# MLP of layer 1 in Strassen products: VectorE's work on the next operand placed behind the running product's first tile, and up product 6 combined through psum

## The chip, the cores and the metric

The kernel runs on one core of one Trainium2 chip. The metric is the device time of one execution in microseconds. The time of the kernel before is the median of three runs.

The engines are called as the profile calls them: PE (TensorE), DVE (VectorE), ACT (ScalarE), POOL (GpSimd) and SP (SyncE, which issues most DMAs). An instruction of an engine waits in that engine's own queue: the engines work beside each other, and each takes its instructions in the program's order.

## What is computed

The program is one inference step of a decoder trunk with two layers. Each layer has a mixer (gated linear attention, then differential attention) and an MLP with a squared ReLU, each followed by a normalized residual. The changed part is the MLP of layer 1, the last long piece of the program:

```python
def post_norm(x, f, g, b):
    return layer_norm(DEEPNORM_ALPHA * x + f, g, b)

def sq_relu_mlp(x, w1, w2):
    h = jax.nn.relu(x @ w1)
    return (h * h) @ w2
...
        x_p = post_norm(x_p, sq_relu_mlp(x_p, mlp_w1[layer], mlp_w2[layer]), ln_mlp_g[layer], ln_mlp_b[layer])
```

`x_p` has 1040 rows of 1024 values (16 meta tokens and 1024 prompt tokens), `w1` is 1024 x 4096 and `w2` 4096 x 1024, all fp32. Eight further rows, the running sequences, go along.

## The kernel before

**Groups and products.** `mlp1` cuts the 4096 hidden values into four groups g of 1024. For each group it computes the hidden values ("up", with w1) and then their part of the output ("down", with w2). Either is a product of two matrices cut into 2 x 2 blocks, and is done with seven block products instead of eight, as Strassen's method does, so some operands are sums or differences of blocks (the tables `UP_W`, `UP_X`, `DOWN_H`, `DOWN_W`; "run" stands for the running sum or difference in `RW` or `RX`). The order is the list `seq`: in each group up products 1, 2, 5, 6, 4, 3, 7, then down products 1, 5, 6, 3, 7, 4, 2 (in the last group 1, 5, 6, 7, 4, 3, 2). That makes 56 products.

**Precision.** Each fp32 operand is split into a rounded part (hi) and a rest (lo), and each product is three matmuls: hi x hi (line L206), hi x lo (L207) and lo x hi (L208), in `mm3`. For the weights (`weight_operand`) ACT writes hi (`whi`, L1634) and POOL subtracts to get lo (`wlo`, L1635); terms of a sum are added by a DMA that POOL issues (L1633), and loads are issued by SP (L1631). For the activations (`chip_operand`) DVE forms the difference of blocks in `RX` (L1609), ACT casts hi (L202), and DVE subtracts hi to get lo (L203); hi and lo go to the tiles `XH`. Both kinds have two buffers, so an operand is written while the product before it runs. `chip_operand` does this in two halves, the inner blocks k = 0 and 1, then k = 2 and 3.

**Tiles.** An up product has four row blocks x two column halves, eight psum tiles of 128 x 258 with 12 matmuls each. `up_tile` then combines a tile with the sums in `HF`: ACT copies for products 1 and 5 (L1682, L1686), DVE adds and subtracts otherwise (L1679, L1680). A down product has four psum tiles of 128 x 512, 12 matmuls each, which `down_tile` adds into `Y`, for products 6 and 7 by way of `RP` (L1710, L1714). The tiles `mmt` and `axt` take turns, three buffers each.

**The running sequences.** Some products carry a "side product" (L1655): four small matmuls that read the fp32 weight tiles, which come free for new loads only after it.

**What sets the order.** The program is recorded in the order of the Python code, with the next product's operands asked for at t = 2 of the running one, and a scheduler then places each engine's instructions by its own estimate of when they are ready. `tc.issue_after(ins)` ties the instructions of its block that run on the engine of `ins` behind `ins`; it adds no wait between engines. So where DVE's steps stand decides, in the scheduler's eyes, when operands are ready, and with that the order of PE's matmuls.

Of the kernel before, what the change touches and what calls it, by code (L numbers as in the profile page):

```python
# [16 lines left out]
ALU = mybir.AluOpType  # L17
# [91 lines left out]
UP_X = {1: [(0, 0)], 2: [(1, 0)], 5: [(0, 1), (0, 0)], 6: [(1, 1), "run"], 4: [(1, 0), "run"], 3: [(1, 1)], 7: [(0, 1), (1, 1)]}  # L109
DOWN_H = {1: [(0, 0)], 2: [(0, 1)], 5: [(1, 0), (1, 1)], 6: [(0, 0), "run"], 3: [(0, 1), "run"], 4: [(1, 1)], 7: [(1, 0), (0, 0)]}  # L110
# [4 lines left out]
def hybrid_step(ctx, tc, A, dbg=None, upto=9):  # L115
    nc = tc.nc
    V, S, G, TE = nc.vector, nc.scalar, nc.gpsimd, nc.tensor
# [24 lines left out]
    def mmt():  # L142
        return banks["mm"].tile([P, 512], F32, name="mmt") if "mm" in banks else pairt()[:, 0]

    def axt():
        return banks["ax"].tile([P, 512], F32, name="axt")

    def smt():
        return banks["sm"].tile([P, 512], F32, name="smt")
# [18 lines left out]
    TH = 512 + NS // 2  # L168
# [29 lines left out]
    def kunit(w, c0):  # L198
        return unit(256, w.rearrange("(k p) n -> p k n", p=P)[:, :, c0 : c0 + 256])

    def split(hi, lo, src, eng=V):
        S.copy(hi, src)  # L202
        return eng.tensor_tensor(lo, src, hi.bitcast(F32), op=ALU.subtract)  # L203
# [139 lines left out]
    ps = smt()  # L343
# [16 lines left out]
    ps = smt()  # L360
# [202 lines left out]
    ps = smt()  # L563
# [4 lines left out]
    ps = smt()  # L568
# [8 lines left out]
    ps = smt()  # L577
# [15 lines left out]
    ps = smt()  # L593
# [5 lines left out]
    for hh in range(2):  # L599
        ps = smt()  # L600
# [13 lines left out]
    ps = smt()  # L614
# [4 lines left out]
    for s in (8, 4, 2, 1):  # L619
        u = t2()[:, :128]  # L620
        level(sb.rearrange("p h t -> p (h t)"), sqk[:, :128], sqk[:, 128:], u, s, V)
        ps = smt()
# [74 lines left out]
    ps = smt()  # L697
# [144 lines left out]
    for h in range(GH):  # L842
        hi, lo = kunit(wi, 2048 + h * 256)
        hv, lv = (w.rearrange("p (k n) -> p k n", n=256) for w in (hi, lo))
        silt = st2.rearrange("p k (c n) -> p k c n", c=2)
        for c in range(2):
            cs = slice(512 * c, 512 * c + 512)
            sil, pts = [], []
            for m in range(2):
                ps = mmt()  # L850
# [218 lines left out]
    steps_v, steps_g = [], []  # L1069
# [171 lines left out]
    for u, t2_ in ((u, t) for u in range(12) for t in range(4)):  # L1241
# [6 lines left out]
        ps = mmt()  # L1248
        for i in range(2):
            t = 2 * t2_ + i  # L1250
# [7 lines left out]
        if u < 8:  # L1258
            tmp = qt.tile([P, 2, 4, 16], F32, name="qr")
# [130 lines left out]
    ps = smt()  # L1390
# [36 lines left out]
    for step in steps + [None] * 0:  # L1427
        if step:
            h, n, t = step
            if h < 7:  # L1430
                if n == 0:
                    nxt = prep(h + 1, *raws[h + 1])
# [14 lines left out]
        at = t % 4 if h == 7 else t // 2  # L1447
        back(t, sc_, po[:, at * P : (at + 1) * P], *vals[h])
        if n % 4 == 3:
            ts = (slice(0, 4), slice(4, 8))[n // 4] if h == 7 else slice(t % 2, 8, 2)  # L1450
            S.copy(Yd[:, ts, h], po.rearrange("p (t e) -> p t e", e=P))
            for i in range(4):
                x = po[:, i * P : (i + 1) * P]
# [30 lines left out]
    HF = hp.tile([P, NB, 2, TH], F32, name="HF")  # L1484

    RX = hp.tile([P, 4 * TH], F32, name="RX")
# [9 lines left out]
    def xr(c):  # L1496
        if c == len(XR):
            XR.append(cp.tile([P, NB, TH], F32, name="XR%d" % c, tag="XL%d" % c))
        return XR[c]
# [40 lines left out]
    XF = [xr(c).rearrange("p k n -> p (k n)") for c in range(2)]  # L1540
# [51 lines left out]
    loads = []  # L1592
    sides = []

    def chip_operand(terms, quarter, n, tmp):


        parts = [x.rearrange("p k n -> p (k n)")[:, : 4 * n] for x in XH.t[count[0] % 2]]
        count[0] += 1
        hi, lo = (x.rearrange("p (k n) -> p k n", n=n) for x in parts)  # L1600
        rv, tv = (x[:, : 4 * n].rearrange("p (k n) -> p k n", n=n) for x in (RX, tmp))
        for j in (0, 2):
            b = slice(j, j + 2)
            x = quarter(*terms[0])[:, b]
            if len(terms) > 1:

                y = rv[:, b] if terms[1] == "run" else quarter(*terms[1])[:, b]
                out = (tv if terms[1] != "run" else rv)[:, b]
                V.tensor_tensor(out, x, y, op=ALU.subtract)  # L1609
                x = out  # L1610
            split(hi[:, b], lo[:, b], x)
        return hi, lo

    def weight_operand(terms, quarter, side=None):
# [29 lines left out]

    w1, w2 = A["mlp_w1"][1], A["mlp_w2"][1]

    def operands(g, up, i):
        if up:
            left = weight_operand(UP_W[i], lambda h, k: (w1, 512 * k, 1024 * g + 512 * h))
            right = chip_operand(UP_X[i], lambda k, c: xr(c)[:, 4 * k : 4 * k + 4, :], TH, RX)  # L1650
            return left, right

        def beside(k, t):
            r, u = beside.quarter
            TE.matmul(acc[u][k * TS : (k + 1) * TS, :], hs[:, 4 * r + k, :], t, start=g == 0 and i in (1, 3), stop=g == 3 and r == 1)  # L1655


        beside.quarter = ({1: (0, 0), 3: (1, 1), 7: (0, 1), 2: (1, 0)} if g < 3 else {1: (0, 0), 5: (0, 1), 6: (1, 0), 7: (1, 1)}).get(i)
        left = chip_operand(DOWN_H[i], lambda c, k: HF[:, 4 * k : 4 * k + 4, c, :512], 512, XF[0][:, : 4 * TH] if g == 3 and i == 7 else RX)
        right = weight_operand(DOWN_W[i], lambda k, u: (w2, 1024 * g + 512 * k, 512 * u), beside if beside.quarter else None)  # L1660
        return left, right

    ups = []
# [8 lines left out]
    def up_tile(g, i, m, c, left, right, ps):  # L1672
        (ah, al), (bh, bl) = left, right
        ps = ps[:, :CH]
        ms, cs = slice(m * P, (m + 1) * P), slice(c * CH, (c + 1) * CH)
        for k in range(4):
            mm3(ps, ah[:, k, ms], al[:, k, ms], bh[:, k, cs], bl[:, k, cs], k == 0, k == 3)
        c11, c12, c21, c22 = (HF[:, 4 * h + m, x, cs] for h in range(2) for x in range(2))
        add = lambda out, x, y: ups.append(V.tensor_tensor(out, x, y, op=ALU.add).ins)  # L1679
        less = lambda out, x, y: V.tensor_tensor(out, x, y, op=ALU.subtract)  # L1680
        if i == 1:
            S.copy(c12, ps)  # L1682
        elif i == 2:
            add(c11, c12, ps)
        elif i == 5:
            S.copy(c22, ps)  # L1686
        elif i == 6:
            less(c21, ps, c12)
            add(c22, c22, c21)
        elif i == 4:  # L1690
            add(c21, c21, ps)
        elif i == 3:
            less(c12, ps, c22)
        else:
            add(c22, c22, ps)
            add(c21, c21, ps)
        if c:
            for h, x in {2: [(0, 0)], 3: [(0, 1)], 7: [(1, 1), (1, 0)]}.get(i, ()):
                hidden(h, x, m)
# [28 lines left out]
    def mlp1():  # L1728
        seq = []
        for g in range(4):  # L1730
            seq += [(g, 1, i) for i in (1, 2, 5, 6, 4, 3, 7)]
            seq += [(g, 0, i) for i in ((1, 5, 6, 3, 7, 4, 2) if g < 3 else (1, 5, 6, 7, 4, 3, 2))]
        nxt = operands(*seq[0])
        n = 0
        for at, (g, up, i) in enumerate(seq):
            now = nxt
            if not up and i == 1:
                if g == 0:
                    beta = alpha_row(A["ln_mix_b"][1:2], ALU.add)
                else:  # L1740
                    for _ in range(2):
                        next(beta, None)
            if at == len(seq) - 2:
                both = {i: now, seq[-1][2]: operands(*seq[-1])}
                for x, t in ((3, 0), (3, 1), (2, 0), (3, 2), (2, 1), (3, 3), (2, 2), (2, 3)):
                    n += 1
                    down_tile(g, x, t, *both[x], axt() if n % 2 else mmt())
                    yield t, int(x == 3)
                return
            for t in range(4):  # L1750
                if t == 2:
                    nxt = operands(*seq[at + 1])
                if t == 1 and sides:
                    side, own = sides.pop(0)
                    for k in reversed(range(4)):
                        side(k, own[k])
                if up:
                    for c in range(2):
                        n += 1
                        up_tile(g, i, t, c, *now, axt() if n % 2 else mmt())  # L1760
                    if g == 0 and at in (1, 2):
                        y = Yt[:, 4 * (at - 1) + t, :]
                        with tc.issue_after(ups[-1]):
                            steps_v.append(V.scalar_tensor_tensor(y, y, ALPHA, grow, ALU.mult, ALU.mult).ins)
                    continue
                n += 1
                down_tile(g, i, t, *now, axt() if n % 2 else mmt())
                if g == 3:
                    for c, u in {7: [(1, 1)], 4: [(1, 0)]}.get(i, ()):
                        yield 4 * c + t, u  # L1770
            if g == 3 and not up and i == 7:
                samples_out()
            if g == 3 and up and i == 7:
                for x, nm in ((fg, "g"), (fb, "b")):
                    dma(x, A["ln_mlp_" + nm][1:2].broadcast_to([P, D]))
                with tc.issue_after(loads[-1]):
                    for t0, t1 in ((0, 2), (4, 8)):
                        dma(A["y_prompt"][0, t0 * P : t1 * P], A["ln_mlp_b"][1:2].broadcast_to([(t1 - t0) * P, D]))
                spare.extend(XF[0][:, 4 * TH + 512 * j : 4 * TH + 512 * (j + 1)] for j in range(4))

    normalize(mlp1(), stats, lambda c: None, last)
    e.close()
    if dbg:
# [27 lines left out]
```

## Time and profile before

| | |
|---|---|
| median of 3 runs | 2797.68 us (2791.86 to 2802.81) |
| the profiled execution | 2808.13 us |
| its span, first to last instruction | 2806.4 us |
| mean granted clock of PE | 0.991 |
| up products of group 0 | from about 2120 us |
| up products of group 1, PE never waiting | 2295.3 to 2375.8 us |
| last products | to about 2793 us, then the last normalization |

The profile comes from one execution. Its page names instructions by line, engine, operation and tiles (out<-in). A row of the view of groups gives the count, the busy time, the mean ns of one, and the idle time of the engine just before them with what ended it. A row of the timeline gives start, duration, engine, line, and in brackets the idle time before it and what released it. In the rows, a matmul's duration is longer than its distance to the next one, since matmuls are pipelined.

### The profile page before, as it was taken

How to read it: one execution, taken by the hardware profiler on the slowest of the kernel's cores; microseconds unless marked ns; L12 is line 12 of the kernel's file. 1: busy time of each engine (PE TensorE's matmuls, PEld its weight loads, DVE VectorE, ACT ScalarE, POOL GpSimd, SP SyncE). 2: the span in 40 equal slices, each digit the busy share in tenths (PEclk: the TensorE clock that was granted, in tenths of full speed). 3: DMA queues.
4: the chain of work that ended last, by engine and by line, in shares of the span. 5: the costliest groups of instructions: out<-in, count | busy, mean ns of one | idle time of the engine just before them, and what ended most of it. 6: DMA issues, size and time to landing. Idle time of an engine off the chain costs nothing. (4 is left out here: it accounts for less than half of the span.)

```text
span 2806.4 us, 52253 instructions
## 1 busy us (share of the span) xinstructions
PE 2726.4 (97%) x19849; PEld 2239.9 (80%) x19849; DVE 1941.7 (69%) x3000; ACT 1114.3 (40%) x2284; POOL 1088.1 (39%) x744
## 2 busy tenths in 40 slices
PE   8989999999999999999999999899999999999998
PEld 5867767987777777777798989777898989798986
DVE  5375362678777787777568740887647888988697
ACT  4324463152221222222242112777625646355554
POOL 2132112234344343434233312200026767666775
PEclk9999999999999999999999999999999999999999
DMA  7476545725798898888658995212144455554575
GB/s 235 166 238 217 198 153 184 261 93 186 284 334 314 310 354 300 334 318 314 243 172 305 361 368 178 65 47 80 38 126 90 103 139 112 140 119 105 133 185 120
DMA packets 276392, 562.81 MB, mean 201 GB/s; under 512 B 23510, under 2 KB 144412, under 8 KB 272044
## 3 DMA queue, kind: packets, MB, share of 16 engines
q1 hardware_dynamic: 256076, 522.75, 53.3%
q0 software_dynamic: 20064, 36.71, 8.0%
q8 instruction: 156, 2.56, 0.4%
q14 instruction: 96, 0.79, 0.1%
HBM read 533.00 MB, written 29.52 MB: 200 GB/s over the span
## 5 line engine op out<-in xcount | busy, mean ns | idle before, releaser
L194 POOL TENSOR_TENSOR wlo<-raw,whi 128x512 fp32r<-128x512 f32 x252 | 360.9, 1446 | 708.7 <-ACT whi L193 586.1
L206 PE MATMUL mmt<-whi,XH 128*128 128x256 f32 (+1 forms) x1760 | 523.9, 300 | 1.1 <-DVE ast L1338 0.9
L207 PE MATMUL mmt<-wlo,XH 128*128 128x256 f32 (+1 forms) x1760 | 522.1, 298 | 0.4 <-POOL wlo L194 0.4
L206 PE MATMUL mmt<-XH,whi 128*128 128x512 f32 (+1 forms) x1216 | 437.4, 361 | 5.9 <-DVE HL L203 2.6
L208 PE MATMUL mmt<-XH,wlo 128*128 128x512 f32 (+1 forms) x1216 | 433.9, 357 | 0.2 <-POOL wlo L1635 0.2
L208 PE MATMUL mmt<-whi,XL 128*128 128x256 f32 x1536 | 432.4, 285 | 0.0
L193 ACT CAST whi<-raw 128x512 fp32r<-128x512 f32 x252 | 150.2, 619 | 567.0 <-PE mmt L208 187.7
L206 PEld LDWEIGHTS mmt<-whi,XH 128*128 128x128 f32 x1760 | 330.5, 189 | 39.7 <-issue 24.3
L943 DVE TENSOR_REDUCE sc<-pg 128x16 f32<-128x1024 f32 x256 | 308.3, 1211 | 69.8 <-POOL pg L942 67.3
L207 PEld LDWEIGHTS mmt<-wlo,XH 128*128 128x128 f32 x1760 | 332.1, 189 | 15.7 <-issue 5.5
L942 DVE TENSOR_TENSOR pg<-pg,qb 128x1024 f32<-128x1024 f32 x192 | 270.7, 1417 | 62.1 <-DMA pg<-in_cache_k 53.5
L207 PE MATMUL mmt<-XL,whi 128*128 128x512 f32 x768 | 308.3, 402 | 0.0
L208 PEld LDWEIGHTS mmt<-whi,XL 128*128 128x128 f32 x1536 | 288.4, 189 | 7.3 <-issue 6.8
L206 PEld LDWEIGHTS mmt<-XH,whi 128*128 128x128 f32 x1216 | 230.6, 190 | 50.2 <-issue 7.6
L942 POOL TENSOR_TENSOR pg<-pg,qb 128x1024 f32<-128x1024 f32 x64 | 163.4, 2555 | 258.3 <-DMA pg<-in_cache_k 175.6
L208 PEld LDWEIGHTS mmt<-XH,wlo 128*128 128x128 f32 x1216 | 231.0, 190 | 36.4 <-issue 3.3
L206 PE MATMUL mmt<-whi,HH 128*128 128x512 f32 x512 | 204.7, 401 | 4.3 <-DVE Y L1175 3.1
L208 PE MATMUL mmt<-whi,HL 128*128 128x512 f32 x512 | 203.9, 398 | 0.0
L207 PE MATMUL mmt<-wlo,HH 128*128 128x512 f32 x512 | 203.4, 397 | 0.0
L1635 POOL TENSOR_TENSOR wlo<-RW,whi 128x512 fp32r<-128x512 f32 x96 | 162.8, 1732 | 69.8 <-ACT whi L1634 69.5
L1635 POOL TENSOR_TENSOR wlo<-rw,whi 128x512 fp32r<-128x512 f32 x92 | 154.4, 1768 | 90.1 <-ACT whi L1634 89.8
L207 PEld LDWEIGHTS mmt<-XL,whi 128*128 128x128 f32 x768 | 146.2, 190 | 39.5 <-issue 8.0
(450 smaller groups left out, 5711.7 us busy)
## 6 DMA issues: line engine op xcount, KB each, us to landing
pg<-in_cache_k SPq DMA_DIRECT2D x256, 512.0 KB
pg<-in_cache_v SPq DMA_DIRECT2D x256, 512.0 KB
raw<-in_mlp_w SPq DMA_DIRECT2D x164, 256.0 KB
swt<-in_mlp_w SPq DMA_DIRECT2D x32, 1024.0 KB
rw<-in_mlp_w SPq DMA_DIRECT2D x116, 256.0 KB
RW<-in_mlp_w POOLq DMA_DIRECT2D x96, 256.0 KB, 5.6
swt<-in_gla_w_in SPq DMA_DIRECT2D x12, 1024.0 KB
swt<-in_diff_w_in SPq DMA_DIRECT2D x12, 1024.0 KB
```

Of the source, the lines that this page charges most:

```text
L193: S.copy(hi[:, c], raw)
L194: G.tensor_tensor(lo[:, c], raw, hi[:, c].bitcast(F32), op=ALU.subtract)
L206: TE.matmul(ps, ah, bh, start=first, stop=False)
L207: TE.matmul(ps, ah, bl, start=False, stop=False)
L208: return TE.matmul(ps, al, bh, start=False, stop=last)
L942: eng.tensor_tensor(pg, pg, qb, op=ALU.mult)
L943: return V.tensor_reduce(sc[:, n, :], pg.rearrange("p (h d) -> p h d", d=64), op=ALU.add, axis=AX.X).ins
L1635: G.tensor_tensor(lo[:, k, :], t, hi[:, k, :].bitcast(F32), op=ALU.subtract)
```

## The change

Two things are changed. First, in up product 6 the difference of a psum tile and a block of `HF` is written back to psum, the second add reads it from there, and a copy brings it to `HF`; before, the difference went to `HF`, and the add read two `HF` blocks. Second, each product gets a mark: the last DVE step of its first row block (none for up products 1 and 5, which have no DVE step). The DVE steps of `chip_operand` for the next product are tied behind that mark. `less` now also records its instruction, so that it can be a mark.

```diff
-    def chip_operand(terms, quarter, n, tmp):
+    def chip_operand(terms, quarter, n, tmp, mark):
...
-                V.tensor_tensor(out, x, y, op=ALU.subtract)
+                with tc.issue_after(mark) if mark else nullcontext():
+                    V.tensor_tensor(out, x, y, op=ALU.subtract)
                 x = out
-            split(hi[:, b], lo[:, b], x)
+            with tc.issue_after(mark) if mark else nullcontext():
+                split(hi[:, b], lo[:, b], x)
...
-        less = lambda out, x, y: V.tensor_tensor(out, x, y, op=ALU.subtract)
+        less = lambda out, x, y: ups.append(V.tensor_tensor(out, x, y, op=ALU.subtract).ins)
...
         elif i == 6:
-            less(c21, ps, c12)
-            add(c22, c22, c21)
+            less(ps, ps, c12)
+            add(c22, c22, ps)
+            V.tensor_copy(c21, ps)
...
             for t in range(4):
+                if t == 1:
+                    mark = ups[-1] if up and i not in (1, 5) else None if up else steps_v[-1]
                 if t == 2:
-                    nxt = operands(*seq[at + 1])
+                    nxt = operands(*seq[at + 1], mark)
```

The order of the instructions moves on DVE and, with it, on PE. **DVE, up product 6 of group 1.** Before, from the last step of product 2 on; `RX` is the difference for the next products, `XH` the operand tiles, and `HF<-axt,HF` the first psum read of a tile of product 6:

```order
L203 TENSOR_TENSOR XH_24052<-RX,XH_86 128x1032
L1609 TENSOR_TENSOR RX<-XR_24892,RX 128x1032
L203 TENSOR_TENSOR XH_24052<-RX,XH_86 128x1032
L1609 TENSOR_TENSOR RX<-XR_24892,RX 128x1032
L203 TENSOR_TENSOR XH_23783<-RX,XH_84 128x1032
L1680 TENSOR_TENSOR HF<-axt,HF 128x258
L1609 TENSOR_TENSOR RX<-XR_25159 128x1032
L1679 TENSOR_TENSOR HF<-HF 128x258
L1680 TENSOR_TENSOR HF<-mmt,HF 128x258
L203 TENSOR_TENSOR XH_23783<-RX,XH_84 128x1032
```

Now, from the first psum read of product 6 on:

```order
L1682 TENSOR_TENSOR axt<-axt,HF 128x258
L1681 TENSOR_TENSOR HF<-HF,axt 128x258
L1692 COPY HF<-axt 128x258
L1682 TENSOR_TENSOR mmt<-mmt,HF 128x258
L1681 TENSOR_TENSOR HF<-HF,mmt 128x258
L1692 COPY HF<-mmt 128x258
L1610 TENSOR_TENSOR RX<-XR_24892,RX 128x1032 x2
L1682 TENSOR_TENSOR axt<-axt,HF 128x258
L1682 TENSOR_TENSOR mmt<-mmt,HF 128x258
L203 TENSOR_TENSOR XH_23783<-RX,XH_84 128x1032
```

Before, both differences for product 4 and the first split stood ahead of the first psum read of product 6; now they stand behind two whole tiles, and the second split of product 4 stands behind five more steps.

**DVE, from down product 5 to down product 6 of group 0.** Before; `RP` is the running sum of product 6, `XH_23783` the lo part of product 3's operand:

```order
L1609 TENSOR_TENSOR RX<-HF,RX 128x1024
L1710 TENSOR_TENSOR Y<-Y,mmt 128x512 x2
L1710 TENSOR_TENSOR Y<-Y,axt 128x512 x2
L203 TENSOR_TENSOR XH_23783<-RX,XH_84 128x1024
L1710 TENSOR_TENSOR Y<-Y,mmt 128x512 x2
L203 TENSOR_TENSOR XH_23783<-RX,XH_84 128x1024
L1609 TENSOR_TENSOR RX<-HF 128x1024 x2
L1710 TENSOR_TENSOR RP<-axt,RP 128x512
L1710 TENSOR_TENSOR RP<-mmt,RP 128x512
```

Now, from the first psum read of product 6 on:

```order
L1713 TENSOR_TENSOR RP<-axt,RP 128x512
L1713 TENSOR_TENSOR Y<-Y,RP 128x512
L1610 TENSOR_TENSOR RX<-HF,RX 128x1024
L1713 TENSOR_TENSOR RP<-mmt,RP 128x512
L1610 TENSOR_TENSOR RX<-HF,RX 128x1024
L1713 TENSOR_TENSOR RP<-axt,RP 128x512
L1713 TENSOR_TENSOR Y<-Y,RP 128x512
L1713 TENSOR_TENSOR RP<-mmt,RP 128x512
L203 TENSOR_TENSOR XH_23783<-RX,XH_84 128x1024
L1713 TENSOR_TENSOR Y<-Y,RP 128x512 x2
L203 TENSOR_TENSOR XH_23783<-RX,XH_84 128x1024
```

The differences and both splits for product 3 stood ahead of product 6's first psum read; now the first split stands behind the psum read of product 6's fourth and last tile.

**PE, start of down product 3 of group 0.** `XH00` is the operand's hi part, `XH01` its lo part, and the first name is the psum tile. Before, one tile is finished before the next is begun:

```order
L206 MATMUL axt_26500<-whi_26452,XH00_84 128x512
L207 MATMUL axt_26500<-wlo_26453,XH00_84 128x512
L208 MATMUL axt_26500<-whi_26452,XH01_23783 128x512
L206 MATMUL axt_26500<-whi_26452,XH00_84 128x512
L207 MATMUL axt_26500<-wlo_26453,XH00_84 128x512
L208 MATMUL axt_26500<-whi_26452,XH01_23783 128x512
```

Now the four tiles are gone through in rounds:

```order
L206 MATMUL axt_26508<-whi_26460,XH00_84 128x512
L207 MATMUL axt_26508<-wlo_26461,XH00_84 128x512
L206 MATMUL mmt_26526<-whi_26460,XH00_84 128x512
L207 MATMUL mmt_26526<-wlo_26461,XH00_84 128x512
L206 MATMUL axt_26576<-whi_26460,XH00_84 128x512
L207 MATMUL axt_26576<-wlo_26461,XH00_84 128x512
L206 MATMUL mmt_26590<-whi_26460,XH00_84 128x512
L207 MATMUL mmt_26590<-wlo_26461,XH00_84 128x512
L208 MATMUL axt_26508<-whi_26460,XH01_23783 128x512
```

Eight matmuls that read hi alone come first, two for each tile; then six for each tile, then four. Most down products are now in such rounds: in product 6 the first tile's twelfth matmul is the 31st of 48 (the 16th before). In product 7 four matmuls of product 4, two with `whi` and two with `wlo`, stand behind the first eight, and product 7's first tile has its twelfth matmul as the 36th of its own, the 40th with those four. The side products that belong to down products 7 and 2 stand inside and at the end of product 3. In up products nearly all tiles are still done one after the other; at the start of up product 4 two tiles share the first 24 matmuls (7, 7, 5, 5).

More of the change, by code (lines that the diff above doesn't have):

```diff
@@ L1645, in hybrid_step, with operands @@
     w1, w2 = A["mlp_w1"][1], A["mlp_w2"][1]
-    def operands(g, up, i):
+    def operands(g, up, i, mark=None):
         if up:
             left = weight_operand(UP_W[i], lambda h, k: (w1, 512 * k, 1024 * g + 512 * h))
-            right = chip_operand(UP_X[i], lambda k, c: xr(c)[:, 4 * k : 4 * k + 4, :], TH, RX)
+            right = chip_operand(UP_X[i], lambda k, c: xr(c)[:, 4 * k : 4 * k + 4, :], TH, RX, mark)
             return left, right
@@ L1658, in operands @@
         beside.quarter = ({1: (0, 0), 3: (1, 1), 7: (0, 1), 2: (1, 0)} if g < 3 else {1: (0, 0), 5: (0, 1), 6: (1, 0), 7: (1, 1)}).get(i)
-        left = chip_operand(DOWN_H[i], lambda c, k: HF[:, 4 * k : 4 * k + 4, c, :512], 512, XF[0][:, : 4 * TH] if g == 3 and i == 7 else RX)
+        left = chip_operand(DOWN_H[i], lambda c, k: HF[:, 4 * k : 4 * k + 4, c, :512], 512, XF[0][:, : 4 * TH] if g == 3 and i == 7 else RX, mark)
         right = weight_operand(DOWN_W[i], lambda k, u: (w2, 1024 * g + 512 * k, 512 * u), beside if beside.quarter else None)
```

## The prediction

> **What bounds the kernel now.** First the page: its span, and the line of busy time.
>
> ```profile
> span 2806.4 us, 52253 instructions
> PE 2726.4 (97%) x19849; PEld 2239.9 (80%) x19849; DVE 1941.7 (69%) x3000; ACT 1114.3 (40%) x2284; POOL 1088.1 (39%) x744
> ```
>
> TensorE (PE) is busy 97% of the time, so the kernel gets faster only where PE waits or runs at a lower clock, and slower wherever PE gets a new wait. The changed code fills the stretch from about 2120 us on. The view of windows, cut at the borders of its "up" (w1) and "down" (w2) products, tells how much PE loses there; the columns are the window, its length, the busy time of five engines, the granted clock, DMA share and rate.
>
> ```profile
> 2150.00:2200.00 50.00, 45.63 (x364) 45.02 (x363) 39.88 (x46) 24.98 (x46) 36.41 (x31) 0.97 0.62 132
> ...
> 2295.30:2375.80 80.50, 80.50 (x674) 80.50 (x673) 62.97 (x79) 50.39 (x97) 62.14 (x44) 1.00 0.49 109
> 2375.80:2458.30 82.50, 82.50 (x370) 63.33 (x369) 76.23 (x70) 35.24 (x57) 55.80 (x44) 1.00 0.58 142
> 2458.30:2543.30 85.00, 81.91 (x674) 81.04 (x673) 68.51 (x80) 50.10 (x97) 57.38 (x44) 1.00 0.46 100
> 2543.30:2625.80 82.50, 82.50 (x369) 63.33 (x369) 67.30 (x69) 35.25 (x57) 55.55 (x44) 1.00 0.58 141
> 2625.80:2706.30 80.50, 80.50 (x674) 80.50 (x673) 61.39 (x78) 49.47 (x96) 62.25 (x44) 1.00 0.69 157
> ```
>
> Seven up products take 80.5 us where PE never waits (groups 1 and 3; 11.5 each), 85.0 in group 2. The down products take 82.5 with PE busy throughout: **there is nothing to win in them**. Their VectorE (DVE) is busy 67 to 76 of 82.5 us, so it has little room. The waits of PE in this part:
>
> ```profile
> PE axt L206 <- DVE HF L1680: 3.7, 1, 3.7
> PE axt L208 <- POOL wlo L1635: 1.9, 2, 1.6
> PE mmt L206 <- DVE HF L1680: 1.2, 1, 1.2
> PE axt L206 <- ACT HF L1686: 0.7, 2, 0.4
> ```
>
> Two of them, 4.9 us, are for psum tiles that DVE has not yet read (L1680, up product 6). The timeline shows how the longer one came about:
>
> ```profile
> 2163.37 8.71 DVE L203 TENSOR_TENSOR XH<-RX,XH 128x1032 fp32r<-128x1032 f32 x1 [3.75 <-ACT XH L202]
> ...
> 2164.46 1.89 POOL L1635 TENSOR_TENSOR wlo<-rw,whi 128x512 fp32r<-128x512 f32 x1
> 2165.70 1.49 POOL L1633 DMA_DIRECT2D RW<-in_mlp_w  x1
> 2166.31 2.20 POOL L1635 TENSOR_TENSOR wlo<-raw,whi 128x512 fp32r<-128x512 f32 x1
> 2167.57 3.41 POOL L1635 TENSOR_TENSOR wlo<-rw,whi 128x512 fp32r<-128x512 f32 x2
> ...
> 2173.74 0.39 PE L206 MATMUL axt<-XH,whi 128*128 128x258 f32 x1 [3.74 <-DVE HF L1680]
> ...
> 2175.20 0.42 PE L208 MATMUL axt<-XH,wlo 128*128 128x258 f32 x1
> ```
>
> A split of the next operand (L203) had both inputs in SBUF and took 8.71 us while POOL subtracted; the psum reads queued behind it, PE ran out of psum tiles, and after the wait its matmuls took 0.42 instead of 0.28 us for a while. Psum reads themselves are never stretched, as the view of groups shows:
>
> ```profile
> L203 DVE TENSOR_TENSOR XH<-RX,XH 128x1024 fp32r<-128x1024 f32 x30 | 60.2, 2006 | 3.1 <-ACT XH L202 3.1
> L203 DVE TENSOR_TENSOR XH<-RX,XH 128x1032 fp32r<-128x1032 f32 x32 | 58.5, 1827 | 30.4 <-ACT XH L202 30.3
> L1609 DVE TENSOR_TENSOR RX<-XR,RX 128x1032 f32<-128x1032 f32 x16 | 37.6, 2350 | 0.3
> L1609 DVE TENSOR_TENSOR RX<-HF,RX 128x1024 f32<-128x1024 f32 x16 | 35.8, 2238 | 0.1
> L1679 DVE TENSOR_TENSOR HF<-HF 128x258 f32<-128x258 f32 x32 | 29.3, 927 | 0.2
> L1679 DVE TENSOR_TENSOR HF<-HF,axt 128x258 f32<-128x258 f32 x64 | 25.2, 415 | 3.6 <-PE axt L208 3.5
> L1710 DVE TENSOR_TENSOR Y<-Y,RP 128x512 f32<-128x512 f32 x16 | 13.3, 845 | 0.2
> L1710 DVE TENSOR_TENSOR RP<-axt,RP 128x512 f32<-128x512 f32 x8 | 5.4, 680 | 1.4 <-PE axt L208 1.4
> L1635 POOL TENSOR_TENSOR wlo<-rw,whi 128x512 fp32r<-128x512 f32 x89 | 150.1, 1778 | 77.8 <-ACT whi L1634 77.6
> L202 ACT CAST XH<-RX 128x1024 fp32r<-128x1024 f32 x30 | 31.5, 1050 | 32.0 <-DVE RX L1609 17.8 <-PE mmt L207 13.6
> ```
>
> **Part 1, up product 6 through psum.** It removes 32 adds with both inputs in SBUF (927 ns mean) and adds 32 with a psum input (415) and 32 copies from psum. No such DVE copy is in the trace; the nearest rows are 415 ns (same size) and 680 (twice the size), so 0.2 to 0.7 us, and I take 0.4, the row of its size. Change in DVE time: 32 x (0.4 + 0.415 - 0.927), about -4 us. A psum tile is held for three steps instead of one, about 0.8 us longer; six tiles of 1.44 us (11.5/8) cover that. The worth for PE is in the two waits.
>
> **Part 2, the marks, in the up products.** The first tile's psum read now comes before the next operand's work, so the wait of 3.7 and the one of 1.2 should go, and with the first the slow matmuls behind it: 16 at twice the pitch of 0.12 us (80.5/674), about 1.6. That gives **-6.5 us**. All that PE loses in group 2 is 4.5 us (85.0 - 80.5), so more than about -10 is not to be had. Given back: the operand of up product 4 (two RX, two L203) now stands among the steps of product 6, as the first piece of order shows. With T the start of product 6, the last split ends at T+11.3 if nothing is stretched (13 psum steps at 0.34 and the tiles' own times up to tile 4, then 4 x 1.15), at T+15 by the group means (2.35, 2.35, 1.83, 1.83); PE needs it at T+11.5 plus 14 matmuls that don't read it, T+13.2. So 0 to 1.8 us a group; I take 1, nearer to the means: +4 in four groups. Up products: **-2.5 us**.
>
> **Part 3, the marks, in the down products.** Here PE had no wait, because the operand was ready long before its use. In group 1:
>
> ```profile
> 2399.47 1.21 DVE L203 TENSOR_TENSOR XH<-RX,XH 128x1024 fp32r<-128x1024 f32 x1
> ...
> 2400.82 4.31 POOL L1635 TENSOR_TENSOR wlo<-rw,whi 128x512 fp32r<-128x512 f32 x3
> ...
> 2401.80 5.68 DVE L203 TENSOR_TENSOR XH<-RX,XH 128x1024 fp32r<-128x1024 f32 x1
> ...
> 2410.27 0.39 PE L206 MATMUL axt<-whi,XH 128*128 128x512 f32 x1
> 2410.50 0.39 PE L207 MATMUL axt<-wlo,XH 128*128 128x512 f32 x1
> ```
>
> Product 3 starts at 2410.27. Its splits ended at 2400.7 and 2407.5: 9.6 and 2.8 us ahead, and the 2.8 covered a stretch by POOL of 4.5 us. The change takes that cover: RX and split of the next product now stand behind the first tile's add. And the orders of PE show that the first tile comes late: PE now goes through the four tiles in rounds (hi parts alone, then the rest), so product 6's first tile is complete at its 31st of 48 matmuls.
>
> *Down product 6 to 3.* T is product 6's start; a matmul costs 0.233 us (2410.27 to 2410.50). First tile complete at T + 31 x 0.233 = T+7.2, read from T+7.5. Then by the second piece of order on DVE: RP, Y, RX, RP, RX, RP, Y, RP, L203. Unstretched (0.6, 0.7, 1.2, 0.6, 1.2, 0.6, 0.7, 0.6, 1.2) the first split ends at T+14.9; by the group means (0.68, 0.845, 2.24, 2.0) at T+18.4. PE is through product 6 at T+11.2 and through the eight matmuls that need hi alone at T+13.1. New wait: 1.8 to 5.3 us; with a stretch like 5.68 for 1.21 in one step, 6.3. I take 4, nearer to the means, since POOL's next subtractions start when product 6's weights come free, at T+11.2, on top of the last steps. Behind it wait PE and, through PE, the loads that refill the tiles of the side product standing inside product 3; the latter I cost at 0 (up to 2).
>
> *Down product 7 to 4.* PE now does four matmuls of product 4 after the first eight of 7. They need wlo of product 4, which comes after 7's start by a cast of XH (1.05), a cast of whi (0.6) and a POOL subtraction (1.78): 3.4, against 10 matmuls, 2.3. **1.1 us** (0 to 2). Then 4's split stands behind 7's first tile: complete at matmul 40 (9.3 + 1.1), four steps (2.7), the split 1.2 to 2.0: 14.6 to 15.4, where PE, through 54 matmuls, is there at 13.7. 0.9 to 1.7, I take **1.2**.
>
> A down group: 4 + 1.1 + 1.2 = 6.3 us; four groups 25. (Lower end 1.8 + 0 + 0.9 = 2.7, so 11; upper 6.3 + 2 + 1.7 + 2 = 12, so 48.)
>
> **Sum**: 25 - 2.5 = +22.5 us on the profiled execution, whose own time is 2808.1 (span 2806.4). That execution is 10.4 above the median of 2797.7, so the difference is put on the median: 2820.
>
> [...]
>
> **The rivals.**
> 1. *The late steps meet no stretch.* For it: after the burst of POOL that a product opens with, POOL is idle (55 to 58 us busy in 82.5). Against: the chain runs on into the next product's burst. Then 1.8 + 1.1 + 0.9 a group, 15, minus 6.5: +9, 2807.
> 2. *Faster: DVE keeps up, only the psum waits go.* Place: the first split of down product 3 and the weights of product 4. It decides if that split ends before T+13.1, for which the first tile must be complete some 2 us earlier than counted. For it: the hi-only round tolerates a late split. Against: 31 of 48 is fixed by the order. Price -6.5 to -10: 2791.
> 3. *The marks move nothing.* The orders exclude it.
>
> **How the numbers follow.** Forecast (slower, +14 to +48): 0.60. Rival 1 (0 to +14): 0.22. Rival 2: 0.18, of which 0.04 for more than -14 us, which would need a gain outside of the waits listed, as in the tail. What a measurement tells from no change is 0.5%, 14 us: faster 0.04, same 0.22 + 0.14 = 0.36, slower 0.60. The range leaves out about 1 in 10 at each end: 2797 to 2846.
>
> **What would show it.** Right: windows of down groups of 87 to 92 us instead of 82.5; new waits of PE for XH L203 at the start of down product 3, for wlo L1637 inside product 7, and for XH in product 4; no more waits for L1682 in the up groups. Part 1: no add HF<-HF, copies of about 0.4 us. Wrong: down groups still near 82.5, or the splits of product 3 ending before PE asks for them. I would be wrong if POOL's subtractions fall elsewhere than after each product's start, or if the tail, which I cost at nothing, moves.

## The result, and the profile after

| | before | changed |
|---|---|---|
| median | 2799.87 us (6 runs, 2791.86 to 2802.81) | 2836.66 us (6 runs, 2830.54 to 2845.6) |
| profiled execution (its span) | 2808.13 us (2806.4) | 2836.58 us (2834.7) |
| ratio of the times | | 1.013, 95% interval 1.0114 to 1.0146 |

The change makes the kernel slower by 36.8 us by the medians, 28.4 by the two profiled executions. The page of the changed kernel, span and busy time:

```profile
span 2834.7 us, 52287 instructions
PE 2733.0 (96%) x19849; PEld 2238.4 (79%) x19849; DVE 1910.9 (67%) x3032; ACT 1112.2 (39%) x2284; POOL 1076.4 (38%) x744
```

DVE does 31 us less work, and the kernel is slower: DVE's busy time is not what sets its length. The view of windows, cut where PE begins an up or a down group (columns as before; down, up, down, up, down, up from group 0 on):

```profile
2207.00:2297.40 90.40, 85.43 (x371) 64.17 (x370) 68.58 (x69) 36.28 (x61) 56.40 (x44) 0.98 0.55 128
2297.40:2380.80 83.40, 81.25 (x674) 80.66 (x673) 64.52 (x88) 48.07 (x93) 58.09 (x44) 1.00 0.50 105
2380.80:2471.20 90.40, 85.44 (x371) 64.13 (x370) 73.18 (x70) 36.78 (x62) 57.08 (x44) 0.98 0.56 130
2471.20:2554.20 83.00, 80.94 (x673) 80.57 (x672) 61.34 (x87) 48.05 (x92) 57.54 (x44) 1.00 0.48 102
2554.20:2644.00 89.80, 85.36 (x371) 64.28 (x370) 66.46 (x68) 36.86 (x62) 54.43 (x44) 0.98 0.55 129
2644.00:2726.50 82.50, 80.99 (x674) 80.61 (x673) 57.79 (x85) 48.32 (x93) 57.19 (x44) 1.00 0.68 147
```

Down groups take 90 us instead of 82.5, and PE is busy 85.4 of them; its clock is at 0.98. Up groups that never waited (80.5) take 82.5 to 83.4. Against the profile before, group by group: the part before the MLP is 3.8 us shorter, the up groups together 1.1 longer, the down groups 28.8 (7.8, 7.8, 7.2, 6.0), and what follows the last down matmul 2.2; together 28.3. The waits of PE in this part:

```profile
PE axt L208 <- DVE XH L203: 14.8, 13, 3.0
PE smt L1586 <- DVE sx L767: 10.9, 1, 10.9
PE axt L206 <- DVE HF L1692: 5.0, 4, 1.8
PE axt L206 <- ACT XH L202: 4.8, 2, 4.2
PE axt L207 <- DVE XH L203: 3.0, 4, 1.7
```

The first and the last are splits of the next operand, for which PE did not wait here in the profile before. L1692 is the new copy of up product 6: PE waits for psum tiles there once in every group. The fourth is in the main one wait of 4.2 us in the last group, for a hi part that ScalarE casts behind weights whose load landed late (ScalarE idle for 7.21 and 1.95 us until two loads had landed, casts of `whi` at 2764.42 and 2767.00; the cast of the hi part at 2767.52). L1586 lies in the tail, when the tiles are done. How the longest wait for a split comes about, in group 1, on DVE:

```profile
2406.55 6.50 DVE L203 TENSOR_TENSOR XH<-RX,XH 128x1024 fp32r<-128x1024 f32 x1
2412.98 1.27 DVE L1713 TENSOR_TENSOR Y<-Y,mmt 128x512 f32<-128x512 f32 x2
2414.34 0.69 DVE L1713 TENSOR_TENSOR RP<-axt,RP 128x512 f32<-128x512 f32 x1
...
2415.68 1.22 DVE L1610 TENSOR_TENSOR RX<-HF,RX 128x1024 f32<-128x1024 f32 x1
...
2417.42 1.22 DVE L1610 TENSOR_TENSOR RX<-HF,RX 128x1024 f32<-128x1024 f32 x1
...
2419.15 1.73 DVE L1713 TENSOR_TENSOR Y<-Y,RP 128x512 f32<-128x512 f32 x1
2420.81 0.68 DVE L1713 TENSOR_TENSOR RP<-mmt,RP 128x512 f32<-128x512 f32 x1
2421.41 1.69 DVE L203 TENSOR_TENSOR XH<-RX,XH 128x1024 fp32r<-128x1024 f32 x1
```

and on PE at the same place:

```profile
2411.46 0.40 PE L208 MATMUL mmt<-whi,XH 128*128 128x512 f32 x1
2413.11 0.50 PE L208 MATMUL axt<-whi,XH 128*128 128x512 f32 x1 [1.25 <-DVE XH L203]
...
2419.82 0.39 PE L207 MATMUL mmt<-wlo,XH 128*128 128x512 f32 x1
2423.15 0.51 PE L208 MATMUL axt<-whi,XH 128*128 128x512 f32 x1 [2.94 <-DVE XH L203]
2423.49 0.58 PE L206 MATMUL axt<-whi,XH 128*128 128x512 f32 x1
2423.87 0.63 PE L207 MATMUL axt<-wlo,XH 128*128 128x512 f32 x1
```

Product 6 starts at 2405.4. Its own second split begins only then, beside POOL's subtractions, and takes 6.50 us, so PE waits 1.25 inside product 6. The first tile's RP follows at 2414.34, then the chain that stands behind the mark, and the split that product 3 needs ends at 2423.10, when PE has stood for 2.94 us. The next ten matmuls, 2423.15 to 2427.14, take 3.99 us instead of 10 x 0.233 (granted clock 0.51 to 0.56 there): 1.7 us more.

### The profile page after: what moved, and what is told of

It is laid out like the page before. It is cut to its first block, busy times and chain, and to the rows that moved or that the text cites. A ratio compares the mean times of both kernels' runs of the same rounds, so it can differ in the third digit from the quotient of the medians.

```text
span 2834.7 us, 52287 instructions
## 1 busy us (share of the span) xinstructions
PE 2733.0 (96%) x19849; PEld 2238.4 (79%) x19849; DVE 1910.9 (67%) x3032; ACT 1112.2 (39%) x2284; POOL 1076.4 (38%) x744
## 4 chain that ended last, share of the span: by engine, by line
PE 76%; DVE 11%; ACT 4%; DMA 3%; issue 3%; POOL 1%; SPq 0%; DVEq 0%; POOLq 0%; ACTq 0%
PE mmt L206 18%; PE mmt L207 18%; PE mmt L208 18%; PE smt L983 4%; PE axt L208 3%; PE axt L207 3%; PE axt L206 3%; DVE XH L203 2%; PE smt L1362 2%; DVE RX L1610 2%; ACT as L1340 1%; DMA swt<-in_mlp_w 1%; PE prt L1336 1%; DVE Y L1713 1%; PE axt L1357 1%
## 5 line engine op out<-in xcount | busy, mean ns | idle before, releaser
L942 DVE TENSOR_TENSOR pg<-pg,qb 128x1024 f32<-128x1024 f32 x192 | 260.3, 1363 | 65.2 <-DMA pg<-in_cache_k 51.5
L1637 POOL TENSOR_TENSOR wlo<-RW,whi 128x512 fp32r<-128x512 f32 x96 | 155.2, 1711 | 95.4 <-ACT whi L1636 95.2
```

Source lines behind the costliest of these rows:

```text
L942: eng.tensor_tensor(pg, pg, qb, op=ALU.mult)
L1637: G.tensor_tensor(lo[:, k, :], t, hi[:, k, :].bitcast(F32), op=ALU.subtract)
```

## The experiments

Each ratio is to the kernel before, on the same chip. "MLP" is the time in the profile from the first up matmul to the last down matmul, and the last columns are lengths of groups 1 to 3 in it, from first matmul to first matmul (down 3 to its last).

| kernel | median us | ratio (95%) | MLP | up 1 | down 1 | up 2 | down 2 | down 3 |
|---|---|---|---|---|---|---|---|---|
| before | 2799.9 | | 672.9 | 80.5 | 82.6 | 84.9 | 82.6 | 86.2 |
| before, profiled again | 2809.9 (one run) | | 670.8 | 80.5 | 82.6 | 81.5 | 82.6 | 87.4 |
| changed | 2836.7 | 1.013 (1.0114 to 1.0146) | 702.9 | 83.4 | 90.4 | 83.1 | 89.7 | 92.2 |
| e1 psum only | 2804.5 | 1.0015 (0.9998 to 1.0031) | 672.9 | 80.5 | 82.6 | 80.5 | 82.6 | 87.3 |
| e2 down marks | 2813.8 | 1.0059 (1.0041 to 1.0078) | 682.5 | 80.5 | 86.9 | 80.5 | 86.3 | 87.8 |
| e3 up marks | 2820.2 | 1.008 (1.006 to 1.01) | 686.6 | 84.1 | 84.5 | 84.7 | 84.0 | 91.8 |
| e4 change without down marks | 2819.9 | 1.0083 (1.0064 to 1.0102) | 689.8 | 84.6 | 84.5 | 83.6 | 86.0 | 91.5 |
| e8 mark of up 6 | 2806.3 | 1.003 (1.0019 to 1.0041) | 676.6 | 82.1 | 82.6 | 83.2 | 82.6 | 86.7 |
| e9 up marks without 6 | 2810.6 | 1.0041 (1.0026 to 1.0057) | 678.0 | 81.6 | 84.5 | 81.6 | 86.3 | 91.3 |
| e7 change, tiles in order | 2810.9 | 1.0043 (1.0029 to 1.0058) | 679.1 | 83.5 | 83.8 | 82.5 | 84.6 | 86.6 |
| e11 down marks, tiles in order | 2805.5 | 1.0024 (1.0014 to 1.0035) | 671.9 | 80.5 | 84.9 | 80.5 | 84.9 | 86.9 |
| e5 change, no POOL subtraction | 2853.5 | 1.0196 (1.0166 to 1.0225) | 720.3 | 80.5 | 98.6 | 80.5 | 97.6 | 99.1 |
| e6 before, no POOL subtraction | 2794.5 | 0.9979 (0.9961 to 0.9997) | 664.8 | 80.5 | 82.7 | 80.5 | 82.7 | 87.2 |
| e10 one split on POOL | 2801.7 | 1.0006 (0.9991 to 1.0022) | 676.5 | 80.5 | 82.6 | 84.9 | 82.6 | 86.6 |

### The parts of the change, one by one

Theory of the first four: the marks of the down products make the loss. e1, the kernel before with

```diff
-            less(c21, ps, c12)
-            add(c22, c22, c21)
+            less(ps, ps, c12)
+            add(c22, c22, ps)
+            V.tensor_copy(c21, ps)
```

> Product 6 of the up products combined through psum (difference, add, copy), without any mark. Theory (the marks of the down products cost the time): no mark, so down groups stay at 82.5 us and the time is within 5 us of before; the two waits of PE for the reads of up product 6 (3.7 and 1.2 us in before) stay about as they were, since the splits still stand ahead of those reads. Rival A (the psum tiles, held for three steps, cost the time): a new wait of about 1.8 us for the copy at the start of up product 4 in each group, so 5 to 8 us above before.

e2, e3 and e4 are the changed kernel with another line for the mark; e2 and e3 also have product 6 as before:

```diff
-                    mark = ups[-1] if up and i not in (1, 5) else None if up else steps_v[-1]
+                    mark = None if up else steps_v[-1]                    # e2
+                    mark = ups[-1] if up and i not in (1, 5) else None    # e3, e4
```

> The marks in the down products alone; the up products and product 6 as before. Theory: the whole loss is here: down groups of about 90 us instead of 82.5, the wait of about 2.9 us for the first split of down product 3 and the matmuls at half clock behind it in each group, 27 to 37 us above before. Rival A (psum tiles held longer) and rival B (the marks of the up products delay the work that the down products start with): half of the loss or less, under 18 us above before.

> The marks in the up products alone, product 6 with its add in SBUF as before. Theory: the waits for the reads of up product 6 shrink (3.7 and 1.2 us in before), some time is given back at the start of up product 4; down groups 82.5 us; 7 us below to 4 us above before. Rival B: the marks of the up products cost 5 us or more, with down groups above 85 us.

> The whole change without the marks in the down products: product 6 through psum, and the marks in the up products. Theory: 6 us below to 5 us above before, and 30 us or more below the changed kernel; down groups 82.5 us; up groups keep the wait of up to 1.8 us at the start of up product 4 that the changed kernel has. Rival A: over 8 us above before.

e1 came out as the theory had it in the main: 0.15% (6.8 us by the medians), an interval that includes no change, and down groups as before. The wait for psum tiles did not stay as it was: in its profile PE waits 6.2 us in group 0, for the new copy, behind a split of 8.64 us. In no other group does it wait for the copy, as rival A would have it. The other three did not come out so. The down marks alone cost 16 us, not 27 or more; the up marks alone cost 22, where a gain or nothing was expected; and the two together, 39, come near the 37 of the change. **So the first theory fell: the up marks cost more than the down marks.** That most of the loss stands in the down groups of the changed kernel does not say that the down marks made all of it: e4 has none, and its four down groups are 11.7 us longer than before (83.7, 84.5, 86.0, 91.5 against 82.6, 82.6, 82.6, 86.2).

The up marks were then split, with product 6 as before in both:

```diff
+                    mark = ups[-1] if up and i == 6 else None                # e8
+                    mark = ups[-1] if up and i not in (1, 5, 6) else None    # e9
```

> Only the operand of up product 4 is held behind the first tile of up product 6; no other mark, product 6 with its add in SBUF. Theory C (this one mark carries the cost of the up marks, through the late splits inside up product 4): 16 to 24 us above before, up product 4 of 12.3 to 16.3 us as with all up marks. Theory D (two parts: the waits inside up product 4, worth about 10 us by the profile of the run with all up marks, and weights that come late for down products 7 and 4, from the other up marks): 6 to 13 us above before, no new waits of over 1 us in the down groups.

> The marks of the up products 2, 4, 3 and 7 without that of product 6; product 6 with its add in SBUF. Theory C: within 4 us of before. Theory D: 8 to 14 us above before; up product 4 at 11.7 us, and in the down groups the waits for weights at products 7 and 4 (1.1 and 4 us in the run with all up marks).

Theory D holds by the times: 6.7 and 11.0 us by the medians, two separate prices that make 18 of e3's 22. In e8 the waits lie in up product 4 (3.1 us with group 0's, 1.4 in each later group), and no down group is longer by more than 0.5 us. They are not the waits of e3, though: in the later groups PE waits in e8 for psum tiles of product 4 that DVE reads late, in e3 for the late split. In e9 up product 4 does not wait, and PE waits in the down groups for weights. The waits of PE in e3, which has both:

```profile
PE axt L207 <- DVE XH L203: 6.6, 7, 1.4
PE axt L206 <- ACT whi L1636: 5.4, 3, 4.0
PE axt L206 <- ACT XH L202: 1.8, 2, 1.0
```

The first row is the late split of up product 4 and of group 2's first product; the second, down product 7 (1.1 and 0.3 us) and product 4 of the last group (4.0), whose weights ScalarE cast late, since their load landed late (ScalarE idle for 6.87 us until it had, cast at 2755.86). How a mark in the up products makes a load of the down products late was read but not isolated: in e9 POOL issued the load that adds the second term to product 7's last piece at 2418.8, 0.9 us ahead of product 7's start; before, at 2418.4, 4.2 us ahead. It stands in POOL's order behind subtractions that need ScalarE's casts of the same weights. These begin 5.7 us after product 3's start in e9 (2412.46 against 2406.80) and 1.0 after it before, behind ScalarE's casts of product 7's operand; and these wait for RX, which DVE ends 3.5 us after product 3's start in e9, behind a split of 7.67 us, and 1.7 us ahead of it before, behind one of 5.68. What made DVE late in the first place is not shown.

### Where TensorE's rounds come in

In e2 PE waits for a split hardly at all (2.8 us in all, at most 0.6), and yet the same marks stand in its down products as in the changed kernel. Two things differ there: down product 6's first tile is complete at its 28th matmul in e2, at its 31st in the changed kernel, and product 6's own second split takes 1.97 us in group 1 instead of 6.50. e7 takes the rounds away: every matmul of a tile is issued behind the last one of the tile before.

```diff
-        for k in range(4):
-            mm3(ps, ah[:, k, ts_], ...)
+        with tc.issue_after(tiles_pe[-1]) if tiles_pe and i not in (3, 2) or g < 3 and tiles_pe else nullcontext():
+            for k in range(4):
+                done = mm3(ps, ah[:, k, ts_], ...)
+        tiles_pe.append(done.ins)
```

> The whole change, and TensorE held to one down tile after the other (in the last group not for the last two products), so that the first tile of a product is complete at its 12th matmul and not at the 31st. Theory (in the down products the loss comes from the first tile being late): the waits for splits at products 6 and 3 shrink from 4.2 to under 2 us a group, no matmuls at half clock behind them; down groups 84 to 88 us instead of 90, 8 to 20 us below the changed kernel, that is 17 to 29 above before. Rival (the chain of operand work behind the mark is too long wherever the first tile ends, and TensorE's rounds only covered for it): as slow as the changed kernel or slower, 35 us or more above before.

e11 is e2 with the same lines:

> The marks in the down products alone (up products and product 6 as before), and TensorE held to one down tile after the other as in the run of the whole change. Theory (a mark in a down product costs something only where TensorE's rounds make the first tile late): down groups of 83 to 84.5 us, 8 us or more below the run with the down marks alone, that is 0 to 8 us above before. Rival (the held operand work costs about the same whatever order TensorE takes): 12 us or more above before.

e7 gives back 26 of the 37 us, more than expected. The first tile is now complete at its 12th matmul; DVE in e7, group 1, where product 6 starts at 2399.0 and product 3 at 2410.1:

```profile
2397.46 2.61 DVE L203 TENSOR_TENSOR XH<-RX,XH 128x1024 fp32r<-128x1024 f32 x2 [0.69 <-ACT XH L202]
...
2402.38 0.68 DVE L1716 TENSOR_TENSOR RP<-axt,RP 128x512 f32<-128x512 f32 x1
2403.09 3.03 DVE L1716 TENSOR_TENSOR Y<-Y,RP 128x512 f32<-128x512 f32 x1
2406.05 2.35 DVE L1610 TENSOR_TENSOR RX<-HF,RX 128x1024 f32<-128x1024 f32 x2
...
2408.92 1.21 DVE L203 TENSOR_TENSOR XH<-RX,XH 128x1024 fp32r<-128x1024 f32 x1
```

The first RP comes 3.4 us after product 6's start, where it came 8.9 after it in the changed kernel; both splits of product 6 are done by 2400.1, ahead of the step that takes 3.03 us (0.69 in the changed kernel, at 2415.07), and the first of product 3 ends as that product starts. PE is busy all of down group 1, clock 1.00:

```profile
2374.40:2458.20 83.80, 83.80 (x370) 63.41 (x369) 71.94 (x72) 37.02 (x62) 58.39 (x44) 1.00 0.59 140
```

e11 against e2: 0.24% above before instead of 0.59%, 7.9 instead of 16.1 us by the medians, as the theory asked; its down groups are 84.9 us, not the expected 83 to 84.5. In the down groups of e11 PE does not wait for a split at all, and in group 1, with as many matmuls as before (82.6 us), it is busy at clock 1.00:

```profile
2362.80:2447.70 84.90, 84.90 (x371) 63.57 (x370) 72.69 (x74) 35.30 (x57) 56.72 (x44) 1.00 0.58 138
```

The 2.3 us come from the order of the side products' 32 matmuls: they stand in four unbroken pieces in the group before, in six in e11, and in five in e7, which is 1.2 us longer. So each further piece costs about 1.15 us, and neither run shows another loss in its group 1. In the last group of the kernel before, a piece of four matmuls takes nearly as long as one of eight: 0.98 us (2720.06 to 2721.04) against 0.99 (2709.15 to 2710.14), and the matmuls at either border stand 0.33 to 0.34 us apart instead of 0.233. e2 has five pieces too; the rest of its 4.3 us there is 0.8 of waits for splits, 1.55 for a weight tile that a side product reads, and smaller steps. Whether the marks or the held order make the further pieces no run shows, since none holds TensorE's order without the marks.

So the waits that a mark in a down product makes come through TensorE's rounds: these put the end of the first tile, behind which the operand is held, late in the product.

### What POOL's part is

e5 is the changed kernel, e6 the kernel before, each with

```diff
-            G.tensor_tensor(lo[:, k, :], t, hi[:, k, :].bitcast(F32), op=ALU.subtract)
+            S.copy(lo[:, k, :], t)
```

> The whole change, with the low parts of the MLP's weights written by a copy on ScalarE instead of the subtraction on POOL, so that the subtraction is left out and POOL does not work beside the splits (the output is not the reference's). Theory: the first tile that comes late and the stretch of splits by POOL both make the waits; without the stretch the waits for splits in the down groups fall from about 5 to under 2.5 us a group, and this kernel stands 8 to 22 us above the next one, which leaves out the same work. Rival (POOL has no part in the loss): 30 us or more above the next one.

> The kernel before with the same copy on ScalarE in place of POOL's subtraction, which is left out (the output is not the reference's). Theory: the wait of 3.7 us in the first up group, made by a split of 8.7 us beside POOL, is gone, no split takes over 2 us, and the time is 3 to 8 us below before. Rival (ScalarE, with 0.6 us more for each piece of weights, becomes late): 5 us or more above before, with waits for weights.

e6 came out as expected, 0.21% faster, and without the wait for psum tiles in up product 6. e5 did not: it is 59 us slower than e6, not 8 to 22. The stretch is gone in it, as the group of splits in e5 shows (before: 2006 ns; the changed kernel: 2068):

```profile
L203 DVE TENSOR_TENSOR XH<-RX,XH 128x1024 fp32r<-128x1024 f32 x29 | 35.3, 1220 | 35.5 <-ACT XH L202 35.5
```

and still PE waits, now for the high parts, inside product 5 and at the start of 6 and 3 of a down group. The row of these waits, and from the timeline the one at the start of product 3 in group 1:

```profile
PE axt L206 <- ACT XH L202: 32.9, 12, 4.1
```

```profile
2436.97 0.40 PE L208 MATMUL mmt<-whi,XH 128*128 128x512 f32 x1
2441.43 0.50 PE L206 MATMUL axt<-whi,XH 128*128 128x512 f32 x1 [4.06 <-ACT XH L202]
```

The edit changed two more things. In group 1 of e5 the first tiles of products 5 and 6 are complete only at the 36th of 48 matmuls. And the copies that it put on ScalarE stand ahead of the cast that product 3 waits for:

```profile
2435.96 1.22 DVE L1610 TENSOR_TENSOR RX<-HF,RX 128x1024 f32<-128x1024 f32 x1
...
2437.21 1.14 ACT L1637 CAST wlo<-rw 128x512 fp32r<-128x512 f32 x2 [9.66 <-issue]
2438.26 0.61 ACT L1637 CAST wlo<-raw 128x512 fp32r<-128x512 f32 x1
2438.78 0.61 ACT L1637 CAST wlo<-rw 128x512 fp32r<-128x512 f32 x1
2439.30 1.13 ACT L1636 CAST whi<-rw 128x512 fp32r<-128x512 f32 x2
2440.34 1.04 ACT L202 CAST XH<-RX 128x1024 fp32r<-128x1024 f32 x1
```

RX is done at 2437.18, and its cast begins 3.2 us later, behind six parts of the next weights, of which the edit added four; in the changed kernel the cast follows RX by 0.1 us (2416.90, 2416.99). So only about 1 us of the 4.06 is left for the late first tile, and e5 does not tell whether the loss needs POOL. The rows of the changed kernel allow an estimate for product 3 in group 1: of the steps behind the mark two are stretched beside POOL's subtractions, Y at 2419.15 (1.73 for 0.69) and the split at 2421.41 (1.69 for 1.22), 1.5 us together. Without them about 1.4 of the 2.94 us would be left. The 1.25 us inside product 6 come with its split of 6.50.

### The wait that the change was to remove

The kernel before, unchanged, for a second profile:

> The kernel before once more, unchanged, for a second profile of it. If the two waits for psum tiles in up product 6 and the 4.5 us of group 2 belong to the kernel, they stand again (3.7 and 1.2 us, group 2 of 85 us); if they belong to the one profiled execution, which was 10 us above the median, group 2 takes 80.5 us and the products of the MLP together about 668 us instead of 673.

The wait of 3.74 us in up product 6 of group 0 stood again, behind a split of 9.00 us; the 4.5 us of group 2 did not (81.5 us, one wait of 0.76), though e10 has them again (84.9). In e1 and e2, whose DVE has the same order there, the split took 8.64 and 8.66; in e11, also with that order, it did not stretch:

```profile
2152.92 1.44 DVE L203 TENSOR_TENSOR XH<-RX,XH 128x1032 fp32r<-128x1032 f32 x1 [4.45 <-ACT XH L202]
```

and that execution took 2795.2 us, where e11's median is 2805.5. So what the marks could win comes in some executions and not in others. Both profiles of the kernel before are of executions some 8 to 10 us above the median; whether the wait of 3.74 us stands in a median one, no profile shows. e10 tries to win it in another way, in the kernel before: the split that had taken 8.71 us goes to POOL. At stake were 3 to 6 us, by the author's estimate: the wait of 3.74 us, and behind it the matmuls of 0.42 instead of 0.28 us.

```diff
-            split(hi[:, b], lo[:, b], x)
+            split(hi[:, b], lo[:, b], x, G if at_first(j) else V)
```

`at_first(j)` is true for the first half of the program's fifth operand alone.

> The kernel before with one instruction moved: the first split of the operand of up product 4 in the first group, the one of 8.71 us, is done on POOL, in POOL's own order. [...] Rival (POOL, which then works longer, brings the low parts of the next weights late): within 2 us of before or above it, with a wait for wlo in up product 4 or 3.

No change that can be measured. In its profile the next split, at 2163.99, took 8.06 us instead, and PE waited 1.9 and 3.3 us for the reads of product 6. No version here that computes the reference's result is faster than the kernel before.

## Why the prediction came out as it did

The direction, the place and the size of the total were right: slower, in the down groups, 28.4 us by the profiles where 22.5 was predicted. That the total came so near is in part luck: the term of the up products had the wrong sign, and that of the down products was reached by losses that were not foreseen.

- **Part 1** held: the copies took 415 ns (0.4 taken), no change of the time can be told (e1). What failed is its cover, "six tiles of 1.44 us cover that". In the changed kernel PE waits 0.6 to 1.8 us for the copy once a group. The hold of 0.8 us was not what mattered: the two RX behind the mark stand in front of most of product 6's reads, and took 6.22 us together in group 1 (2 x 1.2 unstretched):

```profile
2336.56 6.22 DVE L1610 TENSOR_TENSOR RX<-XR,RX 128x1032 f32<-128x1032 f32 x2
2342.70 0.42 DVE L1682 TENSOR_TENSOR axt<-axt,HF 128x258 f32<-128x258 f32 x1
...
2345.18 0.41 DVE L1692 COPY HF<-axt 128x258 f32<-128x258 f32 x1
2345.51 0.41 DVE L1681 TENSOR_TENSOR HF<-HF,mmt 128x258 f32<-128x258 f32 x1
```

- **Part 2, up products, -2.5 us** is the step that failed, by its sign. Alone these marks cost 22 us (e3). By place, the up groups of the changed kernel are 1.1 us longer, not 2.5 shorter. Its gain, -6.5, was read off one execution, and neither wait is in all of them: the 1.2 was missing in the next profile of the same kernel, the 3.7 in e11. What was given back (up product 4, 1 us a group) was near the waits seen there, up to 1.7 us in e4 and in the changed kernel, but the waits for the copy came beside them. And it looked at product 4 alone: the marks behind the up products 2, 4, 3 and 7 were costed at nothing, and by e9 they cost 11 us, in the weights of the down products.
- **Part 3, +25 us** had the mechanism right, the first tile late by the rounds (e7, e11), and half of its size from elsewhere. By group 1 of the changed kernel, in time from start to start of a matmul: product 3 waits 3.1 us (4 taken, 1.8 to 5.3 bounded), product 7 0.3, for its own split and not for wlo as foreseen (1.1), product 4 0.8 (1.2). Not foreseen: 1.4 us inside product 6, by its own split of 6.5 us. Left out of the sum and present: 1.7 us of matmuls at a granted clock of 0.51 to 0.56 behind the wait. Together 7.3 of the 7.8 us that the group lost, where 6.3 had been predicted. But the down marks alone make the four down groups only 13.4 us longer (e2), and the change without them 11.7 (e4): together 25 of the 28.8. With both kinds of marks the first tile ends three matmuls later than in e2, and product 6's second split takes 6.50 us instead of 1.97; which mark makes that is not shown.
- **The tail, costed at nothing**, cost 2.2 us: PE stood 10.9 us for sx at L1586, as in e2, which has the down marks too. With the tiles in order that wait is 0.6 and 0.7 us (e7, e11), so it hangs on the rounds as well.
- **Putting the difference on the median** assumed that the profiled execution's surplus of 10 us would be in both. It was in the kernel before alone, which is 8 of the 14 us between 22.5 and 36.8.
- Rival 1 (no stretch, +9) fails by the rows of the changed kernel: its late steps did meet a stretch, if only of 1.5 us in group 1, and product 6's own split one of 5.3. What the kernel would lose with no stretch stays open, since e5 loads ScalarE instead. Rival 2 (the psum waits go, DVE keeps up) would have needed the first tile early; e7 has it early, and still is 11 us above before, 7 of them in up groups 1 to 3 of its profile.

What stays open: where the delay that an up mark brings to the weights of down products 7 and 4 begins, how much of the loss POOL's stretch makes, and why the medians of e3 and e4 stand 3 to 9 us further above before than the MLP of their profiles does.

## What to carry to other kernels

To hold work behind "the first tile" is a statement about the order of another engine. Before it is priced, look at which matmul of that product ends the tile: where TensorE goes through its tiles in rounds, the first may end when two thirds of the product are done (here at the 31st of 48 matmuls). And look for a wait in a second profile before counting its removal as a gain; and take each of several marks alone, since the group in which the time is lost need not be the one whose mark loses it.

## What was not expected of the hardware

A split on DVE with both inputs in SBUF takes 1.22 us on average in e5, and 2.07 in the changed kernel beside POOL's subtractions. The one of 6.50 us outlasted four of them, which stood one behind the other:

```profile
2406.38 4.34 POOL L1637 TENSOR_TENSOR wlo<-rw,whi 128x512 fp32r<-128x512 f32 x3
2410.13 1.84 POOL L1637 TENSOR_TENSOR wlo<-raw,whi 128x512 fp32r<-128x512 f32 x1
```

It began 0.17 us into the burst. In e2 one that began 0.40 us into the burst at the same place (2399.93 against 2399.53) took 1.97 us, so the start alone doesn't say which it will be; and one program's executions differ in it, as up product 6 of group 0 shows, 8.6 to 9.0 us in four profiles with that order on DVE and 1.4 in the fifth.

The granted clock halved behind shorter waits, too, than the one of 3.74 us before. Behind that one:

```profile
2175.60:2178.20 2.60, 2.60 (x14) 2.60 (x13) 2.60 (x6) 1.19 (x2) 0.00 (x0) 0.50 0.01 1
```

In the changed kernel it was at 0.53 behind a wait of 2.27 us (group 2, product 6), the first row, and at 1.00 behind one of 2.81 us ahead of the MLP (L954, at 1510.02), the second:

```profile
2587.60:2591.00 3.40, 3.40 (x8) 2.69 (x9) 2.39 (x4) 0.00 (x0) 0.70 (x1) 0.53 0.81 174
1510.00:1513.40 3.40, 3.38 (x27) 3.36 (x28) 3.40 (x7) 0.70 (x2) 2.05 (x2) 1.00 1.04 410
```

The length of the wait alone does not decide it.
